# The down projection of a streaming encoder's ConvFFN: sample products in six visits with a ring of nine raw weight tiles, and operands of the second product ahead of the first one's copies

## Chip, cores and metric

One core of one Trainium2 chip. The metric is the device time of one execution in microseconds; the median of three runs is 1355.42 us (1353.54 to 1355.63). Below, PE is TensorE, ACT ScalarE, DVE VectorE, POOL GpSimd and SP the engine whose queue issues nearly all DMAs.

## What is computed

One layer of a hybrid encoder, for 1024 tokens of a new stream (the prompt) and for the next 32 tokens of a running one (the samples). A mixer comes first and a channel mixer, the ConvFFN, last:

```python
def conv_ffn(xn, buf, w_up, conv_w, conv_b, w_down):
    up = xn @ w_up
    up, buf = causal_dwconv(up, buf, conv_w, conv_b)
    gate, val = jnp.split(up, 2, axis=-1)
    return (jax.nn.gelu(gate, approximate=True) * val) @ w_down, buf
...
    h, ffn_buf = conv_ffn(rms_norm(x, g_ffn_pre[l]), states[6][l], ffn_w_up[l], ffn_conv_w[l],
                          ffn_conv_b[l], ffn_w_down[l])
    x = x + rms_norm(h, g_ffn_post[l])
```

The model width is 1024 and the hidden width 2816, that is 22 blocks of 128. All is float32. This case is about the last matrix product, the down projection: a 1024 x 2816 matrix (prompt) and a 32 x 2816 one (samples) by the 2816 x 1024 weights.

## The kernel before

**Precision.** A float32 product is made of three passes: each operand is split into a high half (ACT casts it, line 94) and a low half (DVE subtracts, line 97), and `mm3` (lines 87 to 90) multiplies high by high (L88), high by low (L89) and low by high (L90). The sample products use plain float32 instead, with the raw weights, and need no halves.

**Seven products.** The prompt's down projection is done in 2 x 2 blocks by a scheme of seven products, P1 to P7, instead of eight. They run in the order P2, P1, P4, P6, P5, P7, P3. Each multiplies 512 tokens by 1408 hidden units by 512 columns: `run` (in `down_all`) walks over 11 panels of 128 hidden units (NP = 11), and each panel is 4 banks of 3 passes, 12 matmuls of 128 x 512. P2 collects in four PSUM banks q20 to q23 (one of tag "sx", three of tag "big"), P1 in x0 to x3 (tag "xw", four banks). P2's banks are copied to `ca` at the end (L1702), P1's are added there later.

**The panels' operands.** `down_operands` makes the halves of a panel: of the hidden activations h (P2h0 and so on, four at a time in tag "hop") and of the weights (P2w0 and so on, seven at a time in tag "op"). The activations come back from DRAM: the up projection stores each finished block y0 to y21 to h_d (L1426), and `load_h` loads ht0 to ht21 from there (L1578), ht11 to ht21 for P2 and ht0 to ht10 for P1. ht0 to ht10 lie in a pool (p11) that takes over the space of the up projection's last tiles, the y tiles among them.

**Raw weights.** `down_raw` loads a panel's weights, 128 x 1024 float32 (512 KB), into a raw tile (wrP2_0 and so on, L1565). The raw tiles are a ring: of every six loads two go to one pool and four to another, so the seventh load takes the place of the first, as soon as that one's last reader is done. For P1 and P2 both halves of a raw tile are read by the sample products, and the first half by the casts.

**Sample products.** `sample_products` (L1608) multiplies the 32 samples' hidden activations (`smp_h`) by the raw weights: per panel two matmuls of 128 x 32 by 128 x 512, each of which the hardware runs as two passes. The results of an even and an odd panel lie in four groups of 32 partitions of one bank, s1 for P2 and s2 for P1. `each` in `rows_of` calls it after every odd panel and after the last: six visits for P2 (two panels each, the sixth one panel), and six for P1. s1 is a bank of tag "xw", so x3 has to wait until s1 is copied to `keep` (L1700).

**Order.** Every engine runs its instructions in order. A scheduler places them when the kernel is built, by the order of the code and its own estimate of when inputs are ready; `tc.issue_after(x)` keeps what is made under it behind x on the same engine. SP issues its DMAs one by one, and an issue that waits holds up all behind it. Eight semaphores are used in turn by SP's DMAs, so no more than eight are under way.

Of the kernel before, what the change touches and what calls it, by code (L numbers as in the profile page):

```python
# [8 lines left out]
F32 = mybir.dt.float32  # L9
# [4 lines left out]
ALU = mybir.AluOpType  # L14
# [64 lines left out]
def body(ctx: ExitStack, tc: tile.TileContext, a: dict):  # L79
    nc = tc.nc  # L80
    act, dve, pool, pe, sp = nc.scalar, nc.vector, nc.gpsimd, nc.tensor, nc.sync
# [5 lines left out]
    def mm3(ps, lh, rh, first, last, **kw):  # L87
        pe.matmul(ps, lh[0], rh[0], start=first, stop=False, **kw)  # L88
        pe.matmul(ps, lh[0], rh[1], start=False, stop=False, **kw)  # L89
        return pe.matmul(ps, lh[1], rh[0], start=False, stop=last, **kw)  # L90

    def split(hi, lo, src, eng=None, heng=None):
        if heng is None:
            act.copy(hi, src)
        else:
            heng.tensor_copy(hi, src)
# [8 lines left out]
    psb = ctx.enter_context(tc.tile_pool(name="psb", bufs=3, space=PSUM, reuse_waits="tile"))  # L105
# [218 lines left out]
    def weights(src, pool_, name, shape, tags=("wr", "wh", "wl"), bufs=(3, 4), eng=None, raw=None, heng=None,  # L324
                low=None, kept=False):

        r = raw
        if r is None:
            r = pool_.tile(shape, F32, tag=tags[0], name=f"{name}r", bufs=bufs[0])
            sp.dma_start(r, src)  # L330
        h = pool_.tile(shape, F32R, tag=tags[1], name=f"{name}h", bufs=bufs[1])
        l = pool_.tile(shape, F32R, tag=tags[2], name=f"{name}l", bufs=bufs[1])
        if kept:
            behind["low"] = sp.dma_start(l.bitcast(F32), low.bitcast(F32))
            if heng is None:
# [873 lines left out]
    upper, jks, kept, pgs = [], [], {}, ExitStack()  # L1209
# [320 lines left out]
    praw, ph, EARLY = [], [], 3  # L1530

    NP = NF // 2
# [19 lines left out]
            sorted((2 * i + 3 * t, t, i) for i in range((NP + 1) // 2) for t in range(8))]  # L1552

    wraws = {}

    def down_raw(kind, p):

        key = (kind, p if kind in ("P1", "P2") else p // 2)
        if key in wraws:
            return  # L1560
        own = len(wraws) % 6 < 2
        r = (praw[0] if own else ph[0]).tile([128, 2, 512], F32, tag="raw", name=f"wr{kind}_{p}", bufs=2 if own else 4)
        if kind in ("P1", "P2"):
            f = p + NP * (kind == "P2")
            behind["SP"] = sp.dma_start(r.rearrange("p j n -> p (j n)"), a["w_dn"][f])  # L1565
        else:
            n = min(2, NP - p)
            src = a["w_dn"][NP + p:NP + p + n, :, 512:].rearrange("f p n -> p f n") if kind == "P3" else \
                ws_d[{"P5": 0, "P7": 1, "P6": 2, "P4": 3}[kind]][:, p:p + n, :]
            behind["SP"] = sp.dma_start(r[:, :n, :], src)  # L1570
        wraws[key] = r
# [3 lines left out]
    def load_h(pool_, f):  # L1575
        hts[f] = pool_.tile([128, SEQ], F32, name=f"ht{f}")
        with tc.issue_after(behind["SP"].ins):
            sp.dma_start(hts[f], h_d[f])  # L1578

    def ablk(i, k, p):  # L1580
        h = hts[p + NP * k]
        return h[:, 512 * i:512 * i + 512]

    ASRC = dict(P1=(0, 0), P2=(0, 1), P4=(1, 1), P6=(0, 0), P5=(1, 1), P7=(1, 0), P3=(0, 1))

    def halves_of(src, name, pool_, tag, bufs):
        t = pool_.tile([128, 2, 512], F32R, tag=tag, name=name, bufs=bufs)
        split(t[:, 0], t[:, 1], src, dve)
        return t[:, 0], t[:, 1]

    def down_operands(ph, kind, p, early=False):
        down_raw(kind, p)
        h = halves_of(ablk(*ASRC[kind], p), f"{kind}h{p}", ph, "hop", 4)
        wp = (ph, "hop", 4) if early else (praw[1], "op", 7)
        if kind in ("P1", "P2"):
            r = wraws[kind, p]
            w = halves_of(r[:, 0], f"{kind}w{p}", *wp)
        else:
            w = halves_of(wraws[kind, p // 2][:, p % 2], f"{kind}w{p}", *wp)
        return h, w  # L1600

    def sample_products(ps, k, p):

        with tc.issue_after(behind["PE"].ins):
            for q in range(p - p % 2, p + 1):
                for j in range(2):
                    r = 64 * (q % 2) + DEC * j
                    pe.matmul(ps[r:r + DEC], smp_h[:, q + NP * k, :], wraws["P2" if k else "P1", q][:, j],  # L1608
                              start=q < 2, stop=q >= NP - 2)

    def down_all(ph, pc, begun, late):

        CA = pc.tile([128, 4, 2, 512], F32, name="ca")
# [2 lines left out]
        sp.dma_start(gp, a["grows"][1:2, :].broadcast_to([128, 1024]))  # L1616
        act.activation(gp[:, 512:], gp[:, 512:], AF.Copy, scale=-1.0)
        ssp = late.enter_context(tc.tile_pool(name="p11", bufs=1, side="right", reuse_waits="tile"))

        def w_banks(name):  # L1620
            return [psf.tile([128, 512], F32, tag="sx", name=f"{name}0", bufs=1)] + \
                [psb.tile([128, 512], F32, tag="big", name=f"{name}{i}", bufs=3) for i in range(1, 4)]

        def run(kind, banks, first, last, each=None, n_end=0):
            end = []
            for p in range(NP):
                ops = begun.pop((kind, p), None) or down_operands(ph, kind, p)
                if p >= NP - n_end:
                    end.append((p, ops))
                    continue  # L1630
                h, w = ops
                for i in range(4):
                    c = slice(128 * i, 128 * i + 128)
                    behind["PE"] = mm3(banks[i], (h[0][:, c], h[1][:, c]), w, first and p == 0, last and p == NP - 1,
                                       skip_group_check=True)
                if each:
                    each(p, w)
            return end
# [41 lines left out]
        def scratch(u):  # L1680
            return pc.tile([128, 4], F32, tag="fss", name=f"gss{u}", bufs=9)

        def rows_of(k, bank):

            def each(p, w):
                if p % 2 or p == NP - 1:
                    sample_products(bank, k, p)
                if k:
                    for f in (NP + EARLY + p, p - NP + 6):
                        if 0 <= f < NF and f not in hts:  # L1690
                            load_h(ph if f >= NP else ssp, f)
                elif p + 6 < NP:
                    load_h(ssp, p + 6)
            return each

        s1 = psf.tile([128, 512], F32, tag="xw", name="s1", bufs=4)
        W = w_banks("q2")
        run("P2", W, True, True, rows_of(1, s1))
        keep = pc.tile([128, 512], F32, name="keep")
        act.copy(keep, s1)  # L1700
        for i in range(4):
            act.copy(CA[:, i, 0], W[i])  # L1702

        X = [psf.tile([128, 512], F32, tag="xw", name=f"x{i}", bufs=4) for i in range(4)]
        s2 = psb.tile([128, 512], F32, tag="big", name="s2", bufs=3)
        run("P1", X, True, False, rows_of(0, s2))
        dve.tensor_tensor(keep, keep, s2, op=ALU.add)
        quarter = pc.tile([DEC, 3, 512], F32, name="quarter")
        for b in range(3):
            sp.dma_start(quarter[:, b], keep[DEC * (b + 1):DEC * (b + 2)])  # L1710
# [3 lines left out]
        W = w_banks("q4")  # L1714
# [9 lines left out]
        W = w_banks("q5")  # L1724
# [35 lines left out]
        W = w_banks("q3")  # L1760
# [89 lines left out]
    p4s, p5s, p6s, p7s, p8s, p9s, pxs, phs, late = (ExitStack() for _ in range(9))  # L1850
# [3 lines left out]
    psf = p4s.enter_context(tc.tile_pool(name="psf", bufs=1, space=PSUM, reuse_waits="tile"))  # L1854
# [5 lines left out]
    own = {"c1": pt.tile([128, 256], F32, name="c1_00")}  # L1860
# [7 lines left out]
    X = col_operands(px, q0, 0, parts="B")  # L1868
# [219 lines left out]
```

## Time and profile before

| | |
|---|---|
| runs, us | 1355.63, 1355.42, 1353.54; median 1355.42 |
| profiled execution, us | 1354.02 |
| its span, first to last instruction, us | 1351.2 |
| mean granted clock of TensorE | 0.985 |
| P2's first matmul, us from the span's start | 1112.07 |
| P1's first matmul | 1149.93 |
| P4's first matmul | 1191.69 |
| sample matmuls of the down projection (L1608) | 88 passes, 0.605 us each |

A row of the timeline gives the start, the length, the engine, the line and operation, output <- inputs, and in brackets how long the engine had been idle and what ended that. Buffer numbers are left out: `q` is any of q20 to q23, `x` any of x0 to x3, `wrP` any raw tile of the down projection. SPq is SP's queue of DMA issues; the time in its rows is that of the issue, not of the transfer. The rows of the window view give each engine's busy time in a stretch.

### The profile page before, as it was taken

Reading aid. Unit: us, or ns where it says so; the run is one execution under the profiler, and the core shown is the slowest. Engines: PE = TensorE matmul, PEld = TensorE weight load, DVE = VectorE, ACT = ScalarE, POOL = GpSimd, SP = SyncE. Lnnn points to the kernel's source line nnn. Section 1 sums busy time; section 2 is a strip of 40 time slices with the busy share of each in tenths; the row PEclk is TensorE's granted clock in tenths of the full one; section 3 lists DMA queues with packets and bytes.
Section 4 is the critical chain, followed back from the end, with each engine's and each line's share of the span. In section 5 each row is a group of like instructions: output and inputs, shape, how many; then the busy total and the mean of one; then the engine's idle time right before and its main releaser. Section 6 shows DMA issues by size and latency. Waiting matters only on the chain.

```text
span 1351.2 us, 25580 instructions
## 1 busy us (share of the span) xinstructions
PE 1306.0 (97%) x9896; PEld 1100.5 (81%) x9896; DVE 1012.7 (75%) x1748; ACT 696.9 (52%) x1298; POOL 310.3 (23%) x412
## 2 busy tenths in 40 slices
PE   6999999998999999999999999999999999999997
PEld 6999889998888887767877777777788886678885
DVE  5795659768598678866789677787898875499566
ACT  5555556554575556434755445444455454454552
POOL 4532302145022254222101111140511000010005
PEclk9999999999999989989989999999999999999999
DMA  9699878786779964543536887967575349654435
GB/s 339 236 359 368 281 243 264 270 287 203 272 243 313 331 204 140 165 150 106 186 98 195 265 233 232 259 172 238 120 175 145 98 154 358 256 162 142 142 107 124
DMA packets 134784, 291.73 MB, mean 216 GB/s; under 512 B 29015, under 2 KB 63991, under 8 KB 132535
## 3 DMA queue, kind: packets, MB, share of 16 engines
q1 hardware_dynamic: 121031, 267.03, 58.5%
q0 software_dynamic: 9120, 18.62, 7.6%
q10 hardware_dynamic: 4512, 4.46, 1.0%
q8 instruction: 77, 1.26, 0.4%
q14 instruction: 44, 0.36, 0.1%
HBM read 229.38 MB, written 85.78 MB: 233 GB/s over the span
## 4 chain that ended last, share of the span: by engine, by line
PE 61%; DVE 8%; ACT 2%; DMA 2%; issue 2%; POOL 1%; DVEq 0%; SPq 0%; POOLq 0%; ACTq 0%
PE pux_None L88 4%; PE pux_None L90 4%; PE pux_None L89 4%; PE q L88 3%; PE puw_None L89 3%; PE puw_None L88 3%; PE puw_None L90 3%; PE q L89 3%; PE q L90 3%; PE x L88 2%; PE x L89 2%; PE x L90 2%; PE us L1453 2%; PE zp L88 2%; PE zp L90 2%
## 5 line engine op out<-in xcount | busy, mean ns | idle before, releaser
L1422 DVE SCALAR_TENSOR_TENSOR y<-uu,fconv_sb,y 128x1024 f32<-128x1024 f32 x88 | 118.0, 1341 | 26.9 <-ACT y L1420 26.4
L1419 POOL COPY fhalo<-uu 128x2 f32<-128x2 f32 x44 | 17.2, 391 | 362.8 <-DVE uu L1338 351.2
L90 PE MATMUL zp<-woh,cl 128*128 128x512 f32 (+1 forms) x144 | 57.7, 401 | 1.5 <-DVE cl L1093 1.5
L88 PE MATMUL zp<-woh,ch 128*128 128x512 f32 (+1 forms) x144 | 58.2, 414 | 0.8 <-ACT ch L1092 0.8
L88 PE MATMUL pv<-wt_0h,xh 128*128 128x256 f32 (+1 forms) x192 | 56.2, 293 | 2.7 <-DVE xl L321 1.6
L1420 ACT ACTIVATE y<-uu,fconv_sb 128x1024 f32<-128x1024 f32 x44 | 54.8, 1245 | 7.6 <-DVE uu L1338 7.1
L89 PE MATMUL zp<-wol,ch 128*128 128x512 f32 (+1 forms) x144 | 57.7, 401 | 0.0
L90 PE MATMUL pv<-wt_1h,xl 128*128 128x256 f32 (+1 forms) x192 | 55.2, 287 | 0.0
L88 PE MATMUL pv<-wt_1h,xh 128*128 128x256 f32 (+1 forms) x192 | 54.8, 286 | 0.0
L90 PE MATMUL pv<-wt_0h,xl 128*128 128x256 f32 (+1 forms) x192 | 54.8, 285 | 0.0
L89 PE MATMUL pv<-wt_0l,xh 128*128 128x256 f32 (+1 forms) x192 | 54.6, 284 | 0.0
L89 PE MATMUL pv<-wt_1l,xh 128*128 128x256 f32 (+1 forms) x192 | 54.5, 284 | 0.0
L208 POOL TENSOR_SCALAR hrs<-hss 128x5 f32<-128x5 f32 (+3 forms) x27 | 11.1, 412 | 175.1 <-DVE hss L1002 172.8
L1663 POOL TENSOR_TENSOR gss<-gss 128x1 f32<-128x1 f32 (+1 forms) x9 | 8.5, 944 | 185.7 <-ACT gjk L1656 185.7
L818 DVE COPY_PREDICATED P<-masks_sb,sc 128x352 f32<-128x352 int32 (+3 forms) x53 | 37.8, 714 | 6.2 <-PE sc L731 5.5
L88 PEld LDWEIGHTS pv<-wt_0h,xh 128*128 128x128 f32 x192 | 36.1, 188 | 4.8 <-DVE xl L321 2.2
L88 PEld LDWEIGHTS pv<-wt_1h,xh 128*128 128x128 f32 x192 | 36.3, 189 | 0.7 <-issue 0.6
L209 POOL TENSOR_TENSOR hrs<-hrs,mhalf 128x5 f32<-128x5 f32 (+3 forms) x27 | 36.2, 1341 | 2.3
L89 PEld LDWEIGHTS pv<-wt_0l,xh 128*128 128x128 f32 x192 | 36.2, 189 | 0.2
L90 PEld LDWEIGHTS pv<-wt_1h,xl 128*128 128x128 f32 x192 | 36.2, 188 | 0.3
L90 PEld LDWEIGHTS pv<-wt_0h,xl 128*128 128x128 f32 x192 | 36.2, 189 | 0.2
L89 PEld LDWEIGHTS pv<-wt_1l,xh 128*128 128x128 f32 x192 | 36.2, 189 | 0.1
(1898 smaller groups left out, 4658.8 us busy)
## 6 DMA issues: line engine op xcount, KB each, us to landing
wus<-in_w_us SPq DMA_DIRECT2D x16, 1024.0 KB, 7.7
wrP<-in_w_dn SPq DMA_DIRECT2D x27, 512.0 KB, 4.0
h_d<-y SPq DMA_DIRECT2D x22, 512.0 KB, 6.3
ht<-h_d SPq DMA_DIRECT2D x22, 512.0 KB, 7.6
wt_0r<-in_w_tok SPq DMA_DIRECT2D x21, 512.0 KB, 5.9
wt_1r<-in_w_tok SPq DMA_DIRECT2D x21, 512.0 KB, 6.1
ws_d<-in_w_dn POOLq DMA_DIRECT2D x20, 512.0 KB, 7.9
wrP<-ws_d SPq DMA_DIRECT2D x20, 512.0 KB, 3.9
```

The source lines that it names most:

```text
L88: pe.matmul(ps, lh[0], rh[0], start=first, stop=False, **kw)
L89: pe.matmul(ps, lh[0], rh[1], start=False, stop=False, **kw)
L90: return pe.matmul(ps, lh[1], rh[0], start=False, stop=last, **kw)
L208: pool.tensor_scalar(out, ss, 1.0 / width, eps, op0=ALU.mult, op1=ALU.add)
L209: pool.tensor_tensor(out, out, mhalf[:n, :cols], op=ALU.pow)
L818: dve.copy_predicated(dst, mk.broadcast_to([n, 11, *mk.shape[2:]]), src)
L1419: behind["POOL"] = pool.tensor_copy(fhalo[:, j, :], u[:, SEQ - 2:SEQ])
L1420: act.activation(y, u, AF.Identity, scale=fconv[:, j, 2:3], bias=fconv[:, j, 3:4])
L1422: dve.scalar_tensor_tensor(y, uu[i][:, s:s + SEQ], fconv[:, j, s:s + 1], y, op0=ALU.mult, op1=ALU.add)
L1453: pe.matmul(ps[DEC * q:DEC * q + DEC], smp_x[:, k, :], wus[:, i % RING_S, q, :], start=k == 0, stop=k == 7)
L1663: pool.tensor_tensor(ss[:n, 0:1], ss[:n, 2:3], ss[:n, 3:4], op=ALU.add)
```

## The change

Three things are done.

- **Visits.** A table VISITS_D says after which panel which sample products run: panels 0 to 3 after panel 3, 4 to 7 after panel 7, 8 to 10 after panel 9. That is three visits for P2 and three for P1. Panel 10's raw weights are loaded ahead of the visit after panel 9. s1 and s2 are allocated at their first visit.
- **Ring.** P1's and P2's raw tiles are a ring of nine: two in the pool of two as before, five (instead of four) in the second, and two new ones in the pool p11. Loads 0 to 6 of P2 use the first two pools, loads 7 and 8 the new two, load 9 takes the place of load 0. The later products use a ring of seven.
- **Order at the seam.** The copies of P2's banks to `ca` are made inside P1, after its second panel's matmuls are written, so that the operands of P1's first panels come ahead of them. On ACT and DVE each P1 activation's halves now come behind the cast of the last weights made (`kept["w"]`).

The core of the diff:

```diff
@@ -1552,14 +1550,16 @@
     wraws = {}
+    VISITS_D = {3: range(4), 7: range(4, 8), NP - 2: range(8, NP)}
...
-        own = len(wraws) % 6 < 2
-        r = (praw[0] if own else ph[0]).tile([128, 2, 512], F32, tag="raw", name=f"wr{kind}_{p}", bufs=2 if own else 4)
+        n = len(wraws) % (9 if kind in ("P1", "P2") else 7)
+        pool_, bufs = (praw[0], 2) if n < 2 else (ph[0], 5) if n < 7 else (praw[2], 2)
+        r = pool_.tile([128, 2, 512], F32, tag="raw", name=f"wr{kind}_{p}", bufs=bufs)
...
     def down_operands(ph, kind, p, early=False):
         down_raw(kind, p)
-        h = halves_of(ablk(*ASRC[kind], p), f"{kind}h{p}", ph, "hop", 4)
+        late = tc.issue_after(kept["w"].ins) if kind == "P1" and p else ExitStack()
+        with late:
+            h = halves_of(ablk(*ASRC[kind], p), f"{kind}h{p}", ph, "hop", 4)
...
-    def sample_products(ps, k, p):
+    def sample_products(ps, k, qs):
 
         with tc.issue_after(behind["PE"].ins):
-            for q in range(p - p % 2, p + 1):
+            for q in qs:
...
         ssp = late.enter_context(tc.tile_pool(name="p11", bufs=1, side="right", reuse_waits="tile"))
+        praw.append(ssp)
...
-        def rows_of(k, bank):
+        def rows_of(k, bank, first=lambda: None):
+
+            banks = []
 
             def each(p, w):
-                if p % 2 or p == NP - 1:
-                    sample_products(bank, k, p)
+                if p == 1:
+                    first()
+                if p in VISITS_D:
+                    if p == NP - 2:
+                        down_raw("P2" if k else "P1", p + 1)
+                    banks.append(banks[0] if banks else bank())
+                    sample_products(banks[0], k, VISITS_D[p])
...
+        def leave_q2():
+            for i in range(4):
+                act.copy(CA[:, i, 0], W[i])
+
+        srow = []
         W = w_banks("q2")
-        run("P2", W, True, True, rows_of(1, s1))
+        run("P2", W, True, True, rows_of(1, lambda: sample_bank(psf, "xw", "s1", 4)))
         keep = pc.tile([128, 512], F32, name="keep")
-        act.copy(keep, s1)
-        for i in range(4):
-            act.copy(CA[:, i, 0], W[i])
-
+        act.copy(keep, srow[0])
         X = [psf.tile([128, 512], F32, tag="xw", name=f"x{i}", bufs=4) for i in range(4)]
-        s2 = psb.tile([128, 512], F32, tag="big", name="s2", bufs=3)
-        run("P1", X, True, False, rows_of(0, s2))
-        dve.tensor_tensor(keep, keep, s2, op=ALU.add)
+        run("P1", X, True, False, rows_of(0, lambda: sample_bank(psb, "big", "s2", 3), leave_q2))
+        dve.tensor_tensor(keep, keep, srow[1], op=ALU.add)
```

**Where instructions move.** SP's queue, from the last h tiles of P2 on (wrP2_6 is the raw tile of P2's panel 6, ht20 an activation block, y21 the last block that the up projection stores, gp a row of gains broadcast to all partitions, out_p_fc an output). In brackets are the semaphores that an issue waits for: DMAHW0 to DMAHW7 belong to earlier DMAs, PE, DVE, ACT and POOL to those engines. A DMA waits first for the earlier user of its own semaphore. Before:

```order
L1943 DMA out_p_fc<-fhalo_8918 128x88 [waits DMAHW6_49,Pool_49]
L1565 DMA wrP2_6_12566<-in_w_dn 128x1024 [waits DMAHW7_49,DVE_49,PE_49]
L1578 DMA ht20_12586<-h_d_86 128x1024 [waits DMAHW0_49]
L1565 DMA wrP2_7_12590<-in_w_dn 128x1024 [waits DMAHW1_49,PE_49]
L1565 DMA wrP2_8_12618<-in_w_dn 128x1024 [waits DMAHW2_49,DVE_49,PE_49]
L1565 DMA wrP2_9_12640<-in_w_dn 128x1024 [waits DMAHW3_49,DVE_49,PE_49]
L1426 DMA h_d_86<-y21_12399 128x1024 [waits DMAHW4_49,DVE_49]
L1616 DMA gp_12423<-in_grows 128x1024 [waits DMAHW5_49]
L1565 DMA wrP2_10_12666<-in_w_dn 128x1024 [waits DMAHW6_49,PE_49,Activation_49]
L1565 DMA wrP1_0_12701<-in_w_dn 128x1024 [waits DMAHW7_49,DVE_49,PE_49]
L1578 DMA ht0_12564<-h_d_86 128x1024 [waits DMAHW4_49,DMAHW0_49]
L1578 DMA ht1_12588<-h_d_86 128x1024 [waits DMAHW1_49]
```

Now, from the same place:

```order
L1565 DMA wrP2_6_12562<-in_w_dn 128x1024 [waits DMAHW6_49]
L1578 DMA ht20_12582<-h_d_86 128x1024 [waits DMAHW7_49,Pool_49]
L1957 DMA out_p_fc<-fhalo_8918 128x88 [waits DMAHW0_49,Pool_49]
L1565 DMA wrP2_9_12640<-in_w_dn 128x1024 [waits DMAHW1_49,DVE_49,PE_49]
L1565 DMA wrP2_10_12660<-in_w_dn 128x1024 [waits DMAHW2_49,PE_49]
L1565 DMA wrP1_0_12696<-in_w_dn 128x1024 [waits DMAHW3_49,DVE_49,PE_49]
L1565 DMA wrP1_1_12718<-in_w_dn 128x1024 [waits DMAHW4_49,DVE_49,PE_49]
L1424 DMA h_d_86<-y21_12399 128x1024 [waits DMAHW5_49,DVE_49]
L1618 DMA gp_12423<-in_grows 128x1024 [waits DMAHW6_49]
L1578 DMA ht0_12560<-h_d_86 128x1024 [waits DMAHW7_49]
L1578 DMA ht1_12584<-h_d_86 128x1024 [waits DMAHW5_49,DMAHW0_49]
L1565 DMA wrP2_7_12586<-in_w_dn 128x1024 [waits DMAHW1_49]
```

Before, wrP2_7 stood in front of y21's store; now it stands behind it, behind the four loads that take the places of wrP2_0 to wrP2_3 (their PE waits are for visit 1), and behind ht1, whose wait for DMAHW5 is for y21's store. wrP2_8 stands three rows further, behind ht21 and ht2.

ACT, the casts of P2's last panels (P2w7 the weights of panel 7, P2h10 the activations of panel 10, gp the sign change of half the gains). Before:

```order
L94 CAST P2h9_12642<-ht20_12586 128x512
L94 CAST P2w7_12595<-wrP2_7_12590 128x512
L94 CAST P2w8_12623<-wrP2_8_12618 128x512
L94 CAST P2w9_12645<-wrP2_9_12640 128x512
L1617 ACTIVATE gp_12423<-gp_12423 128x512
L94 CAST P2w10_12671<-wrP2_10_12666 128x512
L94 CAST P1w0_12706<-wrP1_0_12701 128x512
L94 CAST P2h10_12668<-ht21_12614 128x512
```

Now:

```order
L93 CAST P2h9_12642<-ht20_12582 128x512
L1619 ACTIVATE gp_12423<-gp_12423 128x512
L93 CAST P2w7_12591<-wrP2_7_12586 128x512
L93 CAST P2h10_12670<-ht21_12614 128x512
L93 CAST P2w8_12623<-wrP2_8_12618 128x512
L93 CAST P2w9_12645<-wrP2_9_12640 128x512
L93 CAST P2w10_12673<-wrP2_10_12660 128x512
L93 CAST P1w0_12701<-wrP1_0_12696 128x512
L93 CAST P1w1_12723<-wrP1_1_12718 128x512
```

gp's operation now stands ahead of panel 7's cast, panel 10's activations ahead of panel 8's weights, and P1's weights 0 and 1 follow at once.

ACT again, at the seam of P2 and P1 (ca takes P2's banks, keep takes s1). Before:

```order
L1702 COPY ca_12421<-q20_12430 128x512
L1702 COPY ca_12421<-q21_12431 128x512
L1702 COPY ca_12421<-q22_12432 128x512
L1702 COPY ca_12421<-q23_12433 128x512
L94 CAST P1h3_12773<-ht3_12638 128x512
L1700 COPY keep_12690<-s1_12429 128x512
L94 CAST P1h4_12799<-ht4_12664 128x512
L94 CAST P1w1_12728<-wrP1_1_12723 128x512
```

Now:

```order
L93 CAST P1w2_12749<-wrP1_2_12744 128x512
L93 CAST P1h2_12746<-ht2_12616 128x512
L1718 COPY keep_12690<-s1_12505 128x512
L93 CAST P1w3_12771<-wrP1_3_12766 128x512
L1712 COPY ca_12421<-q20_12429 128x512
L1712 COPY ca_12421<-q21_12430 128x512
L1712 COPY ca_12421<-q22_12431 128x512
L1712 COPY ca_12421<-q23_12432 128x512
```

The cast of P1's weights 1 has moved from behind the five copies to ahead of them.

More of the change, by code (lines that the diff above doesn't have):

```diff
@@ L92, in split @@
     def split(hi, lo, src, eng=None, heng=None):
[L93 to L96, printed above, removed]
+        ins = act.copy(hi, src) if heng is None else heng.tensor_copy(hi, src)
         (eng or pool).tensor_tensor(lo, src, hi.bitcast(F32), op=ALU.subtract)
+        return ins
     def tanh(out, in_, scale):
@@ L1587, in halves_of @@
         t = pool_.tile([128, 2, 512], F32R, tag=tag, name=name, bufs=bufs)
-        split(t[:, 0], t[:, 1], src, dve)
+        kept["w"] = split(t[:, 0], t[:, 1], src, dve)
         return t[:, 0], t[:, 1]
@@ L1694, in rows_of, with sample_bank @@
             return each
-        s1 = psf.tile([128, 512], F32, tag="xw", name="s1", bufs=4)
+        def sample_bank(pool_, tag, name, bufs):
+            srow.append(pool_.tile([128, 512], F32, tag=tag, name=name, bufs=bufs))
+            return srow[-1]
+        def leave_q2():
+            for i in range(4):
+                act.copy(CA[:, i, 0], W[i])
+        srow = []
         W = w_banks("q2")
-        run("P2", W, True, True, rows_of(1, s1))
+        run("P2", W, True, True, rows_of(1, lambda: sample_bank(psf, "xw", "s1", 4)))
         keep = pc.tile([128, 512], F32, name="keep")
-        act.copy(keep, s1)
-        for i in range(4):
-            act.copy(CA[:, i, 0], W[i])
+        act.copy(keep, srow[0])
         X = [psf.tile([128, 512], F32, tag="xw", name=f"x{i}", bufs=4) for i in range(4)]
-        s2 = psb.tile([128, 512], F32, tag="big", name="s2", bufs=3)
-        run("P1", X, True, False, rows_of(0, s2))
-        dve.tensor_tensor(keep, keep, s2, op=ALU.add)
+        run("P1", X, True, False, rows_of(0, lambda: sample_bank(psb, "big", "s2", 3), leave_q2))
+        dve.tensor_tensor(keep, keep, srow[1], op=ALU.add)
         quarter = pc.tile([DEC, 3, 512], F32, name="quarter")
```

## The prediction, on record before the run

> **What bounds the kernel now.** The profile's page comes first. TensorE (PE) is busy nearly throughout, so the question is where it idles, and what it does at all in the stretch that the change touches.
>
> ```profile
> span 1351.2 us, 25580 instructions
> PE 1306.0 (97%) x9896; PEld 1100.5 (81%) x9896; DVE 1012.7 (75%) x1748; ACT 696.9 (52%) x1298; POOL 310.3 (23%) x412
> ```
>
> Next, busy time by stretches of the down projection (after the stretch: PE, PEld, DVE, ACT, POOL, granted clock, DMA share, GB/s).
>
> ```profile
> 1122.00:1150.00 28.00, 28.00 (x138) 18.49 (x138) 15.36 (x22) 11.35 (x20) 0.00 (x0) 1.00 0.97 345
> 1150.00:1160.00 10.00, 8.13 (x33) 4.91 (x31) 2.59 (x4) 4.71 (x9) 0.00 (x0) 1.00 1.03 419
> 1160.00:1330.00 170.00, 170.00 (x763) 135.40 (x763) 123.37 (x199) 84.16 (x163) 22.37 (x25) 1.00 0.47 139
> ```
>
> PE idles only at the seam between products P2 and P1, 1.87 us in 1150 to 1160, and never in the 170 us behind it. So whatever this stage gains or loses arrives whole at the end of the span. The DMA engines are as good as full until 1160: loads arrive late here, if anything does. The timeline of PE shows the two waits of the seam.
>
> ```profile
> 1154.88 0.50 PE L88 MATMUL x<-P1w,P1h 128*128 128x512 f32 x1 [0.64 <-ACT keep L1700]
> 1157.07 0.50 PE L88 MATMUL x<-P1w,P1h 128*128 128x512 f32 x1 [1.23 <-ACT P1w L94]
> ```
>
> The first waits for the copy that frees s1's bank, the second for an operand whose cast stands on ACT behind the copies of the banks:
>
> ```profile
> 1153.21 0.62 ACT L1702 COPY ca<-q 128x512 f32<-128x512 f32 x1
> 1154.21 0.62 ACT L1700 COPY keep<-s 128x512 f32<-128x512 f32 x1
> 1156.40 1.13 ACT L94 CAST P1w<-wrP 128x512 fp32r<-128x512 f32 x2
> ```
>
> **The change part by part.** *Visits, 12 to 6.* PE's timeline around a visit of two panels, and around one of the up projection with as many sample matmuls as the new visits have:
>
> ```profile
> 1122.04 0.39 PE L90 MATMUL q<-P2w,P2h 128*128 128x512 f32 x1
> 1122.36 1.07 PE L1608 MATMUL s<-wrP,smp_h 128*32 128x512 f32 x8
> 1123.35 0.50 PE L88 MATMUL q<-P2w,P2h 128*128 128x512 f32 x1
> 1123.69 0.39 PE L89 MATMUL q<-P2w,P2h 128*128 128x512 f32 x1
> ...
> 1124.85 0.39 PE L89 MATMUL q<-P2w,P2h 128*128 128x512 f32 x1
> 1125.08 0.39 PE L88 MATMUL q<-P2w,P2h 128*128 128x512 f32 x1
> ...
> 1152.29 1.05 PE L1608 MATMUL s<-wrP,smp_h 128*32 128x512 f32 x4
> ...
> 739.03 0.39 PE L90 MATMUL puz_None<-T4h,A_3h 128*128 128x512 f32 x1
> 739.35 1.93 PE L1453 MATMUL us<-wus,smp_x 128*32 128x512 f32 x16
> 743.87 0.39 PE L90 MATMUL pux_None<-T2h,S_3h 128*128 128x512 f32 x1
> ```
>
> Undisturbed, wide matmuls follow each other every 0.227 us (1124.85 to 1125.08). From 1122.04 to 1125.08 there are eight steps, 1.81 us; it took 3.04, so a visit costs 1.23 us. From 739.03 to 743.87 there are twelve steps, 2.72 us; it took 4.84: a double visit costs 2.12. Twelve visits cost 14.76 us, six double ones 12.72: **2.04 us saved**. (A visit of one panel, the row with x4, takes 1.05 us for 1.07 of two: a pair's panels run side by side. So I count each as a pair, and a visit of three panels as one of four.)
>
> *The seam.* In the new order ACT casts P1's weights 0 and 1 before the copies, and s1's last visit comes before P2's last panel, so its copy is done before P1's fourth bank is asked for: both waits go, **1.87 us**. Their restarts (0.34 us from 1123.35 to 1123.69 instead of 0.227) cost 0.11 each; two go, one comes below: 0.1. Behind them P1's operands come next, and they have time: with nine raw slots their loads stand earlier on SP.
>
> *The loads.* This is the part that speaks against the change. Visit 1 now comes after panel 3 and frees four raw tiles at once. On SP the loads of P2 panels 9 and 10 and P1 panels 0 and 1 take these slots. Behind them stand the store of the last y21, gp, ht0, and ht1, which waits for the store's landing; only behind ht1 stands the load for **P2 panel 7**, the first of the two in the pool that takes over y's space. Panel 7 is wanted long before panels 9, 10 or anything of P1. Before, its load came soon after visit 0, in front of these. When is it wanted, and when does it land?
>
> PE wants it here:
>
> ```profile
> 1126.98 1.06 PE L1608 MATMUL s<-wrP,smp_h 128*32 128x512 f32 x8
> 1137.51 0.84 PE L88 MATMUL q<-P2w,P2h 128*128 128x512 f32 x3
> ```
>
> 1137.51 is where panel 7 starts now, behind three visits. Afterwards it is behind one double visit: 1137.51 - 3 x 1.23 + 2.12 = 1135.94. Visit 1 itself starts at 1126.98 - 1.23 = 1125.75.
>
> SP and its landings before (the landing of a load is where ACT's wait for it ends):
>
> ```profile
> 1123.45 0.33 SPq L1565 DMA_DIRECT2D wrP<-in_w_dn  x1
> ...
> 1128.08 0.81 SPq L1565 DMA_DIRECT2D wrP<-in_w_dn  x2
> 1128.98 0.38 SPq L1426 DMA_DIRECT2D h_d<-y  x1
> 1129.41 0.42 SPq L1616 DMA_DIRECT2D gp<-in_grows  x1
> 1137.63 3.51 SPq L1578 DMA_DIRECT2D ht<-h_d  x6
> ...
> SPq L1578 <- DMA h_d<-y: 2.0, 1, 2.0
> wrP<-in_w_dn SPq DMA_DIRECT2D x27, 512.0 KB, 4.0
> ```
>
> ```profile
> 1135.07 0.62 ACT L94 CAST P2w<-wrP 128x512 fp32r<-128x512 f32 x1 [0.17 <-DMA wrP<-in_w_dn]
> 1136.32 0.62 ACT L94 CAST P2w<-wrP 128x512 fp32r<-128x512 f32 x1 [0.63 <-DMA wrP<-in_w_dn]
> 1138.85 0.63 ACT L1617 ACTIVATE gp<-gp 128x512 f32<-128x512 f32 x1 [1.91 <-DMA gp<-in_grows]
> 1146.14 0.62 ACT L94 CAST P2h<-ht 128x512 fp32r<-128x512 f32 x1 [3.13 <-DMA ht<-h_d]
> ...
> 1127.08 1.22 DVE L1425 TENSOR_TENSOR y<-y,y 128x1024 f32<-128x1024 f32 x1
> ```
>
> Transfers land in the order of issue, 1.25 us apart when the queue is full: two loads and gp at 1135.07, 1136.32 and 1138.85, with the store of y21 between them at 1137.6 (the row of SP's waits: ht0 waited 2.0 us for it and was issued at 1137.63). 512 KB at the 419 GB/s of 1150 to 1160 is also 1.25 us.
>
> The first load behind visit 0 was issued at 1123.45, 1.09 us after the visit's start. So panel 9's load goes at 1125.75 + 1.09 = 1126.84 and panel 10's 0.43 later (1128.98 to 1129.41 is such a step); P1's two wait for the visit's second half, 0.86 us (1.93 less 1.07): 1127.70 and 1128.13. y21's store follows at 1128.56 (its last product on VectorE, from 1127.08 for 1.22, is done), gp and ht0 by 1129.4: the queue stays full. Panel 9 lands 4.0 us on (the median of its kind) to 7.0 (1128.08 to 1135.07, the slowest near it); y21's store is four tiles further: 1126.84 + 4.0 + 5.0 = 1135.84, or 1138.84. Then ht1 and panel 7 are issued. In front of panel 7 are gp, ht0 and ht1, so it lands 4 x 1.25 = 5.0 us after the store, or 6.0 as ht0 did before, also with three tiles ahead (1137.63 to 1146.14 - 2 x 1.25 = 1143.64, ht21 being two tiles behind it). Bounds: 1140.84 and 1144.84; no row favours either, so I take the middle, 1142.84. The cast and PE's start behind it take 0.7 us (1156.40 to 1157.07 above). PE starts panel 7 at 1143.54 instead of 1135.94: a **stall of 7.6 us**, between 5.6 and 9.6. ACT queues gp's operation, for a transfer that lands earlier, ahead of this cast, and panel 10's h and all later casts behind it; they wait too, but PE is the only one who needs them.
>
> [...] The row above shows 419 GB/s from HBM to this core over 10 us, so the sum goes by 1.25.
>
> *The sum:* 7.6 - 2.04 - 1.87 - 0.1 = **+3.6 us**, bounds +1.6 and +5.6. The profiled execution took 1354.02 us (span 1351.2 and 2.8 around it): 1357.6. It lies 1.4 below the median of the runs, 1355.42; against that, 1359.0. Edits at nothing: the casts' new order within P2 (PE takes 12 x 0.227 = 2.72 us for a panel, ACT 1.13 for two casts), and P4's loads in another order: the first panel's waits for the second visit of P1 and has three panels and a visit, 3 x 2.72 + 2.12 = 10.3 us, for a transfer of 4.0, with DMA share at 0.47 there.
>
> **The rivals.** From the page, one more row of issues (KB, median us to landing):
>
> ```profile
> h_d<-y SPq DMA_DIRECT2D x22, 512.0 KB, 6.3
> ```
>
> *(a) Panel 7 arrives in time, faster.* It needs a landing before 1135.2, 0.7 ahead of 1135.94. With 4.0 us for the load, y21's store would have to land by 1131.2, 2.6 us from its issue, less than half the median of its kind (6.3) and with four loads in front of it on its queue. Then only the savings remain: -4.0, 1351.4 on the median. The side changes at a stall of 4.0 us, a landing at 1139.2.
>
> *(b) The store overtakes the four loads, no change.* If y21 took that median from its issue at 1128.56, it would land at 1134.86; panel 7, issued 0.43 later and landing after 4.0, at 1139.3; stall 4.1, sum +0.1: 1355.5.
>
> Against it: y21's landing in sequence above. [...] In this trace the four transfers of 1135 to 1139 landed in order.
>
> *(c) Panel 8 stalls as well, slower still.* Its load stands behind ht21 and ht2: 3 x 1.25 = 3.75 us after panel 7. PE covers 2.72 + 2.12 = 4.84 with panel 7 and visit 2. At the 7.0 us that a load took at 1128, 3 us come on top of the 3.75, 1.9 more than the cover: +5.5, 1360.9; with the longest stall 1362.9.
>
> **How the numbers follow.** Forecast 0.63, (a) 0.12, (b) 0.15, (c) 0.10. The time is 1359.0. The forecast's own range is 1355.1 (the lowest run, 1353.54, and 1.6) to 1361.2 (the highest, 1355.63, and 5.6). To hold 8 in 10 it is extended down over (b), 1353.54 + 0.1, and up over most of (c): 1353.5 to 1362.0. 0.2% of this kernel, about what its measurement can tell from no change, is 2.7 us. The bounds +1.6 to +5.6 lie beyond it for 2.9 of 4.0 parts: slower 0.63 x 0.72 + 0.10 = 0.55; same 0.63 x 0.28 + 0.15 = 0.33; faster 0.12.
>
> **What would show it.** Right: PE's list of waits has a new first row for the stretch, q L88 for ACT P2w, of 5.6 to 9.6 us near 1136 to 1144; ACT's cast before it waits for DMA wrP; SP's waits show ht for DMA h_d<-y of some 7 us; six rows of sample matmuls, up to 16 long, at 2.1 us each; and no PE wait at the P2-P1 seam. Wrong: panel 7's matmuls follow panel 6's without a gap, or the gap is below 4 us; or PE waits in P1 or P4, where I expect none.

## The result, and the profile after

The changed kernel takes 1358.89 us (median of 22 runs, 1352.94 to 1363.27), the kernel before 1355.22 us beside it (22 runs, 1348.74 to 1360.19). The ratio is 1.0032 with a 95% interval of 1.0020 to 1.0044: slower by 4.3 us, between 2.7 and 6.0 (the two medians lie 3.7 us apart). The profiled execution took 1357.25 us.

The page's first lines: PE is busy 2.5 us less than before (1306.0), the span is 4.1 us longer.

```profile
span 1355.3 us, 25578 instructions
PE 1303.5 (96%) x9896; PEld 1101.9 (81%) x9896; DVE 1013.6 (75%) x1748; ACT 698.1 (52%) x1298; POOL 309.1 (23%) x412
```

PE's waits from 1100 to 1345 (line, what was waited for: us in total, times, longest). Both rows of the seam are gone, and one new one stands in their place:

```profile
PE q L88 <- ACT P2w L93: 6.8, 1, 6.8
```

SP's queue around it, and SP's wait for the store of y21. The ht row holds two issues, ht0's and ht1's; 6.2 of its 7.08 us are ht1's wait for that store. Panel 7's load is the single wrP right behind it, at 1136.03.

```profile
1126.05 1.76 SPq L1565 DMA_DIRECT2D wrP<-in_w_dn  x4
1127.89 0.47 SPq L1424 DMA_DIRECT2D h_d<-y  x1
...
1128.91 7.08 SPq L1578 DMA_DIRECT2D ht<-h_d  x2
1136.03 0.43 SPq L1565 DMA_DIRECT2D wrP<-in_w_dn  x1
```

```profile
SPq L1578 <- DMA h_d<-y: 6.2, 1, 6.2
```

ACT's timeline: the cast of panel 7's weights waits for that load and starts as it lands; panel 10's activations, weights 8 to 10 and P1's follow.

```profile
1136.88 0.63 ACT L1619 ACTIVATE gp<-gp 128x512 f32<-128x512 f32 x1 [3.64 <-DMA gp<-in_grows]
1141.48 0.62 ACT L93 CAST P2w<-wrP 128x512 fp32r<-128x512 f32 x1 [3.96 <-DMA wrP<-in_w_dn]
...
1145.24 1.66 ACT L93 CAST P2w<-wrP 128x512 fp32r<-128x512 f32 x3 [1.85 <-DMA wrP<-in_w_dn]
```

PE's timeline, from visit 1 to visit 2:

```profile
1124.95 1.92 PE L1610 MATMUL s<-wrP,smp_h 128*32 128x512 f32 x16
...
1134.91 0.39 PE L90 MATMUL q<-P2w,P2h 128*128 128x512 f32 x1
1142.15 2.07 PE L88 MATMUL q<-P2w,P2h 128*128 128x512 f32 x4 [6.85 <-ACT P2w L93]
1144.02 0.63 PE L89 MATMUL q<-P2w,P2h 128*128 128x512 f32 x1
1144.44 0.63 PE L90 MATMUL q<-P2w,P2h 128*128 128x512 f32 x1
...
1147.44 1.92 PE L1610 MATMUL s<-wrP,smp_h 128*32 128x512 f32 x16
```

Look at the starts behind the wait, not only at the wait: they are 0.42 us apart (1144.02 to 1144.44) and a row lasts 0.63 us instead of 0.39. Panel 7 takes 5.29 us (1142.15 to 1147.44). The busy time by stretches, with the granted clock in the third column from the right, says why:

```profile
1138.00:1140.00 2.00, 0.00 (x0) 0.00 (x0) 0.00 (x0) 0.00 (x0) 0.00 (x0) 1.00 0.94 379
1140.00:1141.00 1.00, 0.00 (x0) 0.00 (x0) 0.00 (x0) 0.00 (x0) 0.00 (x0) 0.70 0.92 340
1141.00:1142.00 1.00, 0.00 (x0) 0.00 (x0) 0.00 (x0) 0.52 (x1) 0.00 (x0) 0.50 1.02 406
...
1143.00:1145.00 2.00, 2.00 (x6) 1.52 (x6) 0.69 (x1) 0.39 (x1) 0.00 (x0) 0.50 1.01 410
...
1147.00:1148.00 1.00, 1.00 (x10) 0.26 (x12) 1.00 (x3) 1.00 (x3) 0.00 (x0) 0.88 0.98 393
1148.00:1150.00 2.00, 2.00 (x19) 0.78 (x12) 1.59 (x3) 0.45 (x1) 0.00 (x0) 1.00 1.03 420
```

PE's clock fell to half while PE stood still and stayed there until 1147.2, so that panel 7 ran at half speed. This the prediction did not have.

**The yardstick of what follows.** The start of P2 lies anywhere between 1106.8 and 1113.6 us in the ten traces, whatever was edited (the earliest is two_behind, whose profiled execution was the fastest of its twelve). So positions are compared from there: the *stretch* from P2's first matmul to P4's first, and the *step* from the start of visit 1 to the start of visit 2 (rows of 16 sample passes). The stretch was 79.62 us before (1112.07 to 1191.69) and is 84.70 now (1111.26 to 1195.96): +5.08 us, within the interval of the ratio. A stretch is that of one profiled execution; the two of the changed kernel differ by 0.19 us.

| kernel | stretch, us | against before | step, us | wait before panel 7 | ratio to before, 95% interval |
|---|---|---|---|---|---|
| changed | 84.70 | +5.08 | 22.49 | 6.85 | 1.0032 (1.0020 to 1.0044) |
| changed_again | 84.51 | +4.89 | 22.14 | 6.38 | 1.0028 (1.0014 to 1.0042) |
| two_behind | 84.40 | +4.78 | 21.92 | 6.14 | 1.0030 (1.0014 to 1.0045) |
| filled_wait | 83.13 | +3.51 | 20.87 | 6.51 filled + 1.23 | 1.0025 (1.0009 to 1.0041) |
| four_behind | 78.29 | -1.33 | 15.89 | 2.60 | 0.9990 (0.9972 to 1.0008) |
| visits_alone | 78.28 | -1.34 | 13.00 | none | 0.9984 (0.9968 to 1.0001) |
| late_slots | 77.55 | -2.07 | 13.00 | none | 0.9992 (0.9974 to 1.0010) |
| seam_alone | 77.17 | -2.45 | twelve visits | none | 0.9988 (0.9974 to 1.0001) |
| late_casts | 75.25 | -4.37 | 13.00 | none | 0.9971 (0.9956 to 0.9986) |

Each ratio is to the kernel before, run in the same series. By whole-kernel times the first four are slower than the kernel before and late_casts is faster; the intervals of the other four include no change, so what is said of them rests on their traces.

### The profile page after: what moved, and what is told of

It is laid out like the page before. It is cut to its first block, busy times and chain, and to the rows that moved or that the text cites. A ratio compares the mean times of both kernels' runs of the same rounds, so it can differ in the third digit from the quotient of the medians.

```text
span 1355.3 us, 25578 instructions
## 1 busy us (share of the span) xinstructions
PE 1303.5 (96%) x9896; PEld 1101.9 (81%) x9896; DVE 1013.6 (75%) x1748; ACT 698.1 (52%) x1298; POOL 309.1 (23%) x412
## 4 chain that ended last, share of the span: by engine, by line
PE 63%; DVE 8%; DMA 2%; ACT 2%; issue 2%; POOL 1%; DVEq 0%; POOLq 0%; SPq 0%; ACTq 0%
PE pux_None L88 4%; PE pux_None L90 4%; PE pux_None L89 4%; PE puw_None L88 3%; PE puw_None L90 3%; PE puw_None L89 3%; PE q L88 2%; PE q L89 2%; PE q L90 2%; PE x L88 2%; PE x L90 2%; PE x L89 2%; PE zp L90 2%; PE zp L88 2%; PE zp L89 2%; PE us L1451 2%
## 5 line engine op out<-in xcount | busy, mean ns | idle before, releaser
L206 POOL TENSOR_SCALAR hrs<-hss 128x5 f32<-128x5 f32 (+3 forms) x27 | 10.1, 375 | 174.8 <-DVE hss L1000 171.9
L1000 DVE TENSOR_REDUCE hss<-sq 128x5 f32<-128x320 f32 (+3 forms) x27 | 13.6, 502 | 30.8 <-ACT sq L999 30.8
```

Source lines behind the costliest of these rows:

```text
L206: pool.tensor_scalar(out, ss, 1.0 / width, eps, op0=ALU.mult, op1=ALU.add)
L1000: dve.tensor_reduce(ss[:n, h0:h0 + nh], sq3, axis=mybir.AxisListType.X, op=ALU.add)
```

## The experiments

My theory: panel 7's load comes late because on SP it stands behind y21's store, and the store behind four loads. Rivals: the store is slow by itself; the DMA engines are full, so that some panel is late in any order. For the slow matmuls: the clock, or their operands.

**four_behind** and **two_behind**: the same nine tiles, with four or two of the loads issued behind panel 8's instead of ahead of the store.

```diff
-            behind["SP"] = sp.dma_start(r.rearrange("p j n -> p (j n)"), a["w_dn"][f])
+            with tc.issue_after(behind["SP"].ins) if p + NP * (kind == "P1") in range(9, NP + 2) else ExitStack():
+                behind["SP"] = sp.dma_start(r.rearrange("p j n -> p (j n)"), a["w_dn"][f])
```

(In two_behind the condition is `kind == "P2" and p > 8`.)

> The changed kernel with the same ring of nine, but the loads of P2's panels 9 and 10 and P1's 0 and 1 are issued behind panel 8's, so that none of the four stands ahead of y21's store; panel 7's load still stands behind the store, gp, ht0 and ht1. All of the work is done. Theory A (panel 7 is late because four tiles of 1.25 us each land ahead of y21's store): the store lands 5 us earlier, and the wait before panel 7 shrinks from 6.85 us to 1 to 2 us; too short for the clock to drop, so -3.9 + 1.0 to 2.0 = -1.9 to -2.9 us against before (ratio 0.998 to 0.9986). Rival C (the store is slow by itself, as the median of 6.3 us of its kind from issue to landing says, and the four loads in front cost little): store issued at about 1127.5 lands at 1133.8, panel 7 5.4 to 5.9 us later, and the wait is still 4 to 5 us; ratio about 1.000.

> The changed kernel, but only the loads of P2's panels 9 and 10 are issued behind panel 8's; P1's 0 and 1 still stand ahead of y21's store. All of the work is done. Theory A: two tiles fewer in front of the store, 2 x 1.25 = 2.5 us; the wait before panel 7 shrinks from 6.85 to 4.3 us. Whether the clock then drops is open: in the changed kernel it dropped 5.1 us after PE had stopped, so by that row a wait of 4.3 us leaves it at 1.00, and the time is -3.9 + 4.3 = +0.4 us against before (ratio 1.0003); if it drops at 4.3 us as well, about 2.4 us more (ratio 1.002). Rival C (store slow by itself): wait 5 us or more, hardly less than 6.85.

Measured, four_behind: SP's wait for the store, SP's timeline with the store's issue and the ht row behind it, and PE's timeline:

```profile
SPq L1579 <- DMA h_d<-y: 1.2, 1, 1.2
```

```profile
1126.05 0.32 SPq L1424 DMA_DIRECT2D h_d<-y  x1
...
1126.90 2.31 SPq L1579 DMA_DIRECT2D ht<-h_d  x2
```

```profile
1123.48 1.92 PE L1611 MATMUL s<-wrP,smp_h 128*32 128x512 f32 x16
1136.43 1.20 PE L88 MATMUL q<-P2w,P2h 128*128 128x512 f32 x4 [2.60 <-ACT P2w L93]
1139.37 1.92 PE L1611 MATMUL s<-wrP,smp_h 128*32 128x512 f32 x16
```

The same three views of two_behind:

```profile
SPq L1579 <- DMA h_d<-y: 4.3, 1, 4.3
```

```profile
1122.40 0.81 SPq L1566 DMA_DIRECT2D wrP<-in_w_dn  x2
1123.31 0.38 SPq L1424 DMA_DIRECT2D h_d<-y  x1
...
1124.21 5.59 SPq L1579 DMA_DIRECT2D ht<-h_d  x2
```

```profile
1120.45 1.92 PE L1611 MATMUL s<-wrP,smp_h 128*32 128x512 f32 x16
1136.95 2.08 PE L88 MATMUL q<-P2w,P2h 128*128 128x512 f32 x4 [6.14 <-ACT P2w L93]
```

The store lands where ht1's issue, the last 0.4 us of the ht row, begins. From its own issue that is 7.7 us with four loads in front (1127.89 to 1128.91 + 7.08 - 0.4 = 1135.6), 6.1 with two (1123.31 to 1129.4) and 2.8 with none (1126.05 to 1128.8). So the store is not slow by itself; that rival falls. From the start of visit 1 the store lands at 10.6, 9.0 and 5.3 us.

The wait before panel 7 shrank less than expected. With two loads fewer, 1.7 us were gained at the store instead of 2.5, because the first load in front is now P1's, which waits for the visit's second half: it is issued 1.95 us behind the visit's start (1120.45 to 1122.40) instead of 1.10 (1124.95 to 1126.05). And panel 7 landed later behind the store: ACT's cast of it starts 5.9 us behind the store's landing in the changed kernel (1135.6 to 1141.48), 6.9 in both of these (1129.4 to 1136.28, 1128.8 to 1135.76). Other executions with the changed kernel's order have 5.5 (changed_again) and 6.1 (filled_wait), so a part may be spread. In that time the DMA engines moved 389 GB/s in the changed kernel and 366 and 335 in these two; why they moved less, no run tells.

**late_slots**: P2's loads 7 to 10 take the places of loads 0 to 3, the two tiles in y's space go to P1's first panels, and P1's loads stand behind the activations' that were made before.

```diff
-        n = len(wraws) % (9 if kind in ("P1", "P2") else 7)
+        i = len(wraws)
+        n = (7, 8, 4, 5, 6, 0, 1, 2, 3)[(i - NP) % 9] if kind == "P1" else i % 7
...
-            behind["SP"] = sp.dma_start(r.rearrange("p j n -> p (j n)"), a["w_dn"][f])
+            with tc.issue_after(behind["h"].ins) if kind == "P1" else ExitStack():
+                behind["SP"] = sp.dma_start(r.rearrange("p j n -> p (j n)"), a["w_dn"][f])
...
-            sp.dma_start(hts[f], h_d[f])
+            behind["h"] = sp.dma_start(hts[f], h_d[f])
```

> The changed kernel, but P2's loads 7 to 10 take the places of loads 0 to 3 (ring of seven), the two new tiles in y's space go to P1's panels 0 and 1, and P1's loads stand behind the activation loads made before them. All of the work is done. Theory A (my forecast: the wait before panel 7 comes from where its load stands on SP, behind y21's store): panel 7's load goes at visit 1, where panel 9's went in the changed kernel (1126.05, landing 1129.7 to 1133), and PE wants it at 1135.3. No wait before panel 7, no half clock behind it, no wait at the seam; what is left are the savings of the visits and of the seam, -3.9 us against before (ratio 0.997). Rival B (the DMA engines are full in this stretch, so that some panel comes late whatever the order): a wait of 3 us or more stands before panel 8, 9, 10 or P1's first panels, and the ratio is at or above 1.000.

Measured: no wait in P2, and one before P1, which ACT's timeline explains:

```profile
1124.73 1.92 PE L1612 MATMUL s<-wrP,smp_h 128*32 128x512 f32 x16
1137.73 1.92 PE L1612 MATMUL s<-wrP,smp_h 128*32 128x512 f32 x16
1152.19 1.20 PE L88 MATMUL x<-P1w,P1h 128*128 128x512 f32 x4 [2.01 <-ACT P1w L93]
```

```profile
1149.57 2.05 ACT L1714 COPY ca<-q 128x512 f32<-128x512 f32 x4 [1.74 <-DMA wrP<-in_w_dn]
1151.48 0.65 ACT L93 CAST P1w<-wrP 128x512 fp32r<-128x512 f32 x1
```

Panel 7 is in time once its load stands ahead of the store, with the store still behind four loads. The wait of 2.01 us, which the expectation did not have, is a new one: with P1's loads moved back, the scheduler put the cast of P1's weights 0 behind the four copies, which wait for P2's end. (The bracket names a load as what ended ACT's idle time. But the first copy starts 0.08 us behind the end of the first of P2's last four matmuls, 1149.10 + 0.39, and late_casts below shows that the order on ACT was the cause.) With its restart the wait took back 2.3 us of the saving.

**late_casts**: late_slots, and the copies behind the cast of P1's weights 1.

```diff
         def leave_q2():
-            for i in range(4):
-                act.copy(CA[:, i, 0], W[i])
+            with tc.issue_after(kept["w"].ins):
+                for i in range(4):
+                    act.copy(CA[:, i, 0], W[i])
```

> The kernel of the run late_slots, with one thing more: the four copies of P2's banks stand on ACT behind the cast of P1's weights 1, so that no cast of P1's first two panels waits for P2's end. All of the work is done. Theory A: the 2.01 us that PE waited before P1 there were ACT's order alone (P1's weights 0 had landed, and their cast stood behind the copies); the wait goes, nothing takes its place, and from P2's first matmul to P4's first it takes 77.55 - 2.01 = 75.5 us (before 79.62, changed kernel 84.70), ratio to before 0.997. Rival B (the DMA engines are full until 1160, and some panel comes late in any order): a wait of 1 us or more stands before another of P1's first four panels, and the stretch takes 76.5 or more.

Measured: PE has no wait in the list from 1100 to 1345. The cast of P1's weights 0 starts 1.34 us before PE wants P1:

```profile
1148.04 0.62 ACT L93 CAST P1w<-wrP 128x512 fp32r<-128x512 f32 x1 [0.85 <-DMA wrP<-in_w_dn]
```

```profile
1149.38 1.07 PE L88 MATMUL x<-P1w,P1h 128*128 128x512 f32 x4
```

The stretch is 75.25 us, the median 1350.10 us against 1353.07 before in the same series, the ratio 0.9971 (0.9956 to 0.9986). This version beats both kernels; the changed one, run in the same series, took 1358.06. So full DMA engines do not make some panel late in every order. That rival falls too.

**filled_wait**: the changed kernel, with 28 idle matmuls behind panel 6.

```diff
+                if k and p == 6:
+                    idle = psf.tile([128, 512], F32, tag="xw", name="idle", bufs=4)
+                    with tc.issue_after(behind["PE"].ins):
+                        for m in range(28):
+                            pe.matmul(idle, w[0][:, :128], w[0], start=True, stop=True)
```

> The changed kernel, with 28 more matmuls of 128 x 512 of panel 6's weights by themselves (28 x 0.227 = 6.36 us) behind panel 6, into a bank that nobody reads; they only keep PE at work while panel 7's load is under way. Theory D (the doubled spacing of panel 7's matmuls, 0.427 us instead of 0.227, is the granted clock, which fell to 0.50 during the wait because PE stood still): granted clock 1.00 throughout, panel 7's twelve matmuls take 2.7 us instead of 5.2, and the kernel is about 2.4 us faster than the changed kernel though it does more: from about +4.3 to about +1.9 us against before (ratio 1.0014). Rival E (panel 7's matmuls were slow because of their operands, DVE's low halves or the casts coming late, or the full DMA engines): the spacing stays at 0.43 behind the filling too, and the ratio stays at 1.003. [...]

Measured, PE's timeline and one stretch:

```profile
1137.49 6.51 PE L1697 MATMUL idle<-P2w 128*128 128x512 f32 x28
1145.23 1.19 PE L88 MATMUL q<-P2w,P2h 128*128 128x512 f32 x4 [1.23 <-ACT P2w L93]
1146.26 0.40 PE L89 MATMUL q<-P2w,P2h 128*128 128x512 f32 x1
...
1148.18 1.92 PE L1610 MATMUL s<-wrP,smp_h 128*32 128x512 f32 x16
```

```profile
1122.00:1150.00 28.00, 26.77 (x132) 19.07 (x130) 12.14 (x17) 10.26 (x18) 0.00 (x0) 1.00 0.98 366
```

Panel 7 waits longer here (7.7 us, filled and not, from 1137.49 to 1145.23; counted alike it was 7.0 in the changed kernel), with the same loads under way, and yet takes 2.95 us (1145.23 to 1148.18) at a clock of 1.00 instead of 5.29 at 0.50. So the slow matmuls were the clock, not operands or DMA traffic. In the four_behind trace the wait of 2.60 us left the clock at 1.00 and panel 7 took 2.94 us (1136.43 to 1139.37). The kernel was expected 2.4 us faster than the changed one. Its stretch is 1.57 shorter: the clock's share went, but the wait was 0.7 longer. The whole-kernel times of the two overlap; the trace decides this, not they.

**visits_alone** and **seam_alone**: the kernel before with one part of the change (in seam_alone the copies are tied behind the cast of P1's weights 1, as in late_casts). Only the main lines of the edits are shown.

```diff
+    VISITS_D = {3: range(4), 7: range(4, 8), NP - 2: range(8, NP)}
...
-                if p % 2 or p == NP - 1:
-                    sample_products(bank, k, p)
+                if p in VISITS_D:
+                    if p == NP - 2:
+                        down_raw("P2" if k else "P1", p + 1)
+                    sample_products(bank, k, VISITS_D[p])
```

```diff
...
-        h = halves_of(ablk(*ASRC[kind], p), f"{kind}h{p}", ph, "hop", 4)
+        with tc.issue_after(kept["w"].ins) if kind == "P1" and p else ExitStack():
+            h = halves_of(ablk(*ASRC[kind], p), f"{kind}h{p}", ph, "hop", 4)
...
+        def leave_q2():
+            with tc.issue_after(kept["w"].ins):
+                for i in range(4):
+                    act.copy(CA[:, i, 0], W[i])
```

> The kernel before with six visits instead of twelve, and nothing else: ring of six, order at the seam as it was. All of the work is done. If the visits save what two rows of the profile before gave for them, PE's work in the stretch from P2's first matmul to P4's first falls by 2.04 us, from 79.62 to 77.6, as long as no load is late. Theory A (a raw slot is freed later by a rarer visit, so the rarer visits need the larger ring): panel 10's load takes the place of load 4, which visit 2 now frees, lands at about 1146 and is wanted by visit 3 at 1145.3; a wait of 1 to 2 us before visit 3 or panel 10, and more at the seam, where P1's weights 0 come later too: 79 to 81 us. Rival (the ring is no matter): 77.6 us, ratio 0.9985.

> The kernel before with the new order at the seam alone (P1's operands ahead of the copies of P2's banks, the copies behind the cast of P1's weights 1; banks s1 and s2 given out after panel 1), twelve visits, ring of six. All of the work is done. By the two waits of the profile before: the 1.23 us for the cast of P1's weights go, the 0.64 us for the copy that frees s1's bank stay, since s1's last visit still comes after panel 10: 79.62 - 1.23 - 0.11 = 78.3 us from P2's first matmul to P4's first, ratio 0.999. Rival: P1's weights 1, whose load stands behind the activations on SP, come no earlier than their cast did, so the wait stays: 79.6.

Measured, visits_alone:

```profile
1150.35 1.05 PE L1609 MATMUL s<-wrP,smp_h 128*32 128x512 f32 x4 [2.15 <-DMA wrP<-in_w_dn]
...
1154.75 1.20 PE L88 MATMUL x<-P1w,P1h 128*128 128x512 f32 x4 [0.41 <-ACT P1w L94]
```

With a ring of six the last visit waits 2.15 us for panel 10's raw weights: the rarer visits do need more raw tiles, as the theory said. The seam's two waits do not appear here either; the last visit now comes before panel 10, which is likely the reason. So by the terms below the stretch should be at -4.37 + 2.15 + 0.41 + 2 x 0.29 = -1.2 us, and it is at -1.34 (78.28 us, less than the 79 to 81 expected). seam_alone, PE and ACT around the former wait for s1's bank:

```profile
1151.14 0.96 PE L90 MATMUL x<-P1w,P1h 128*128 128x512 f32 x3
1151.94 0.46 PE L88 MATMUL x<-P1w,P1h 128*128 128x512 f32 x1
```

```profile
1151.25 0.59 ACT L1710 COPY keep<-s 128x512 f32<-128x512 f32 x1 [6.13 <-PE s L1610]
```

Both waits of the seam are gone, not one: with the bank copies moved back, s1's copy is the first thing that ACT does behind the last visit. The seam is worth 2.45 us, more than the 1.87 of the two idle times. The expectation of 78.3 us was too high.

**changed_again**: no edit.

> The changed kernel once more, unchanged. If the two parts of its loss are of the kernel and not of one execution: a wait of 6.5 to 7.5 us before panel 7, the granted clock at 0.50 for some 5 to 7 us from the end of the wait on, about 84.7 us from P2's first matmul to P4's first, and a ratio of 1.003. If the clock's fall was chance: clock 1.00 behind the wait, 82.3 us, ratio 1.0015.

Measured: the wait and the half clock are there again.

```profile
1124.07 1.92 PE L1610 MATMUL s<-wrP,smp_h 128*32 128x512 f32 x16
1140.79 2.08 PE L88 MATMUL q<-P2w,P2h 128*128 128x512 f32 x4 [6.38 <-ACT P2w L93]
1146.21 2.09 PE L1610 MATMUL s<-wrP,smp_h 128*32 128x512 f32 x16
```

```profile
1142.00:1145.00 3.00, 3.00 (x9) 2.32 (x8) 0.95 (x2) 1.14 (x3) 0.00 (x0) 0.50 1.02 416
```

The other executions agree. Half clock for 6.83 us takes 0.0025 off the mean granted clock of the whole kernel (6.83 x 0.5 / 1355). That mean is 0.983 in the changed kernel (22 executions), 0.984 in changed_again and 0.983 in two_behind (12 each), and 0.986 or 0.987 in every other kernel, filled_wait and the kernel before (35 and 32 executions) included.

## Why the prediction came out as it did, step by step

The direction and the mechanism held: a saving at the visits and the seam, and a larger loss because panel 7's load fell behind y21's store. The sizes were off in both directions, and one term was missing.

- **Visits, -2.04.** late_casts has the whole saving and no new wait, -4.37; seam_alone has -2.45 of it. That leaves -1.92 for the visits. Right.
- **Seam, -1.87 and -0.1.** It is -2.45. The step that failed is the price of the restarts. A wait costs more than its idle time, since the idle time counts from the end of the last row, 0.39 us behind its start, while the next start was due after 0.227; and the first matmuls behind it are slow as well (a row of four takes 1.20 us behind a wait, 1.07 without). The step from visit 1 to visit 2 shows it: 13.00 us without a wait, 15.89 in four_behind with an idle time of 2.60 and full clock, so 2.89 for 2.60. That is 0.29 us a wait where I had 0.1.
- **The loads.** The order on SP and its consequence were as forecast, wait for the store included (7.08 us for the two ht issues). From the start of visit 1, 1125.75 in the forecast and 1124.95 here: the store lands at 10.6 us (forecast 10.1 to 13.1), the cast of panel 7 starts at 16.5 (its landing was forecast at 15.1 to 19.1, the middle 17.1), PE was due to start it at 10.2 (1134.91 + 0.227 = 1135.14), as forecast.
- **The wait, 7.6.** Counted as in the forecast, from the start that was due, it is 1142.15 - 1135.14 = 7.0 us (6.85 of it in the row as idle time) and 0.5 less in changed_again, inside the bounds of 5.6 and 9.6. The term was too large by 0.6 to 1.1 us, because I took the middle between two bounds and the store landed near the early one; the time from there to panel 7 was near its late bound and took back 0.4.
- **Missing: the clock behind the wait.** I priced panel 7 at 12 x 0.227 = 2.72 us. At half clock it took 5.29, against 2.94 in four_behind: 2.35 us that the sum did not have. The profile before could have warned of it: TensorE's longest wait there, its start aside, is 2.5 us, and yet the granted clock fell seven times ahead of the end (the last section has one).
- **The sum, +3.6.** With the measured terms: -1.92 - 2.45 + 6.85 + 0.29 + 2.35 = +5.1 us; the stretch shows +5.08. The visits' term is itself a difference of two stretches, but the last three stand alone: the changed kernel's stretch is 9.45 us longer than late_casts', and 6.85 + 0.29 + 2.35 = 9.49. By the stretch the forecast was 1.5 us short: the half clock left out 2.35, and a wait 0.5 too long and a seam 0.5 too cheap took back most of the rest. That +3.6 lies so near to the measured +4.3 (between 2.7 and 6.0) is in part luck.
- **Rival (a)**, panel 7 in time, falls by the wait itself. What it promised, -4.0 us, is what late_casts gives (-4.37) with the load in another place.
- **Rival (b)**, the store overtakes the loads, falls: with four loads in front the store landed 7.7 us after its issue, with none 2.8.
- **Rival (c)**, panel 8 late as well, falls: its cast starts at 1145.24, 2.2 us before visit 2 and over 4 us before PE wants it. I had taken its load 3.75 us behind panel 7's, which holds (1141.48 to 1145.24).
- **The rate of the transfers.** From 1141 to 1150 the stretches of 1 or 2 us, those not shown above included, have 377 to 434 GB/s, 399 to 422 over 2 or 3 us, as before; only from 1138 to 1141, behind ht1's wait, do they show 379 and 340. So the sum was right to go by 419 GB/s, 1.25 us for a tile of 512 KB.
- **P4's loads and the casts' order in P2, at nothing.** PE has no other wait up to 1345.

## What to carry to other kernels

A freed buffer is an offer to every load that comes next in the queue: before giving out more buffers at once, look at which loads will take them, what stands behind these on the issuing queue, and which of it is needed first. Here giving the early slots to the next panels and the new tiles to the later product, and with that the first casts of P1 ahead of the copies, turned +0.3% into -0.3%. When a wait of a few us is weighed, price the work behind it at half clock too (panel 7 took 5.29 us here instead of 2.94), and price a small wait at more than its idle time (2.89 us here for 2.60).

## What the runs showed of the hardware beyond what was expected

- **The fall.** A wait of 6.1 to 6.9 us halved TensorE's granted clock in all three profiled executions that had it. The fall came 5.1 us after PE's last matmul in the changed kernel (1135.30 to 1140.41), 5.3 in two_behind and 5.3 in changed_again. At half clock the matmuls of 128 x 512 start 0.427 us apart (1144.02 to 1147.01 in the changed kernel, seven steps) instead of 0.227.
- **The length of a wait does not decide alone.** Waits of 2.60 us (four_behind), 2.15 (visits_alone) and 2.01 (late_slots) left the clock at 1.00. But in the kernel before, in an earlier stage, one of 2.45 us was followed by half clock, 3.1 us after it began:

```profile
676.26 0.38 PE L88 MATMUL puw<-T1h,S_0h 128*128 128x256 f32 x1 [2.45 <-ACT T1h L1249]
```

```profile
673.46:676.87 3.41, 0.73 (x4) 0.33 (x3) 2.45 (x5) 3.41 (x8) 0.00 (x0) 1.00 1.04 112
676.87:683.70 6.83, 5.55 (x18) 4.45 (x19) 6.76 (x11) 2.23 (x5) 0.00 (x0) 0.50 0.06 1
```

  In the same kernel the clock fell at 417.46 behind a wait of 2.15 us (413.23 to 415.38). So the full clock behind four_behind's 2.60 us gives no safe size. What decides besides the length, no run here isolates.
- **How long half clock lasts.** In the traces of the kernel before and of the changed kernel the clock fell seven times each ahead of the end, and half clock lasted 3.41 us (four times and three) or 6.83 us (three times and four). It lasted 6.83 us in the three waits of this case (1140.41 to 1147.24 in the changed kernel, 1136.15 to 1142.98 in two_behind, 1139.77 to 1146.60 in changed_again), though PE was at work again 1.74, 0.80 and 1.02 us after the fall. In each of the two traces the falls lie whole multiples of 3.413 us apart (417.46 to 676.87 in the kernel before: 259.41 us, 76 times; 676.20 to 1140.41 in the changed kernel: 464.21 us, 136 times).
